# Seven products instead of eight for more weight pairs, with two of the four weight sums made by transfers in DRAM

## The chip, the cores and the metric

One core of a Trainium2 chip runs the whole program. The metric is the device time of one execution in microseconds (us). The engines: TensorE (PE, its weight loads listed as PEld), VectorE (DVE), ScalarE (ACT), GpSimd (POOL) and SyncE (SP), each with an instruction queue of its own that it works off in order. Here nearly all DMAs that load weights are issued by SP, the others by POOL.

## The reference

One layer of a decoder trunk on x of 256 tokens x 2048, all in float32:

```
h  = rmsnorm(x);  z = h @ w_in          # q, k, v, gates of both kinds of heads
A  = forgetting attention (8 heads);  M = mLSTM (4 heads)
x  = x + (sigmoid(g_a) * (A @ w_proj_a) + sigmoid(g_m) * (M @ w_proj_m)) @ w_out
h2 = rmsnorm(x);  u = causal_dwconv(h2 @ w_up)      # 2 x 5632 columns
x  = x + (silu(u_gate) * u_val) @ w_down            # 5632 -> 2048
```

## The kernel before, in words

*Precision.* Each float32 operand is split into a part `wh` that the matmul's input type holds and a rest `wl`. A product takes three matmuls: rest x wh, high x wh, high x wl (`prod`, L302). The splitting of the weights runs while the matmuls run: ACT copies a piece of up to 1024 columns into `wh` (L176), DVE subtracts to get `wl` (L177). Both have four buffers (L174, L175).

*Loading.* All weight matrices are one list of chunks [128, up to 2048], loaded by SP in that order into three buffers `raw` (`load_chunk`, L130). `subs_of` cuts each chunk into pieces; `split_sub(j)` (L140) makes piece j, `next_sub` (L184) hands it to the matmuls and splits one to three pieces ahead of them. The up product, the queries and the keys use chunks with two "whole" pieces.

*Pairs of seven products.* The products with the values (`w_v`, two blocks of 1024 columns), all gates (`w_g`, four blocks), the output weight (`w_out`, two) and the last product (`w_dn`, two blocks named y0 and y1) go by pairs of 128 contraction rows: 2 x 128 rows, 2 x 128 tokens and 2 x 512 columns make a 2 x 2 block product (`s_block`, L295). A pair of kind "p" does it with eight products of three matmuls, a pair of kind "S" with seven, by the Strassen-Winograd scheme: sums of the four weight blocks and sums of the four activation blocks come in, sums of the products come out. The pattern of a block is a string (L36 to L39): "pSpSpSpp" for eight pairs, "p" + "Sp" * 10 + "p" for the 22 pairs of the last product.

For an S pair the four weight sums are made on DVE from the loaded chunk: a wide one of 1024 columns (L161, both halves at once), then two of 512 (L168, L171). Its pieces are b (1024 columns), b21 (512), t13 and t24 (1024 each, out of the sums), and the matmuls take them in that order, 6, 3, 6 and 6 matmuls.

*Sums of the activations.* They are made once (`put_sums`, L226). For the values and gates they stay in SBUF (`sums`, L638, done during the key product); for the last product they are written to DRAM during the up product (L961) and come back in a ring of tiles `s_ops` for two pairs each (L971), on POOL's queue.

*Order.* The code's order is the order of each engine's queue except where the tool that builds the program finds an instruction ready earlier in its own estimate of the times, and queues it ahead. `tc.issue_after(x)` keeps what follows behind x on that engine's queue (used at L160 and L507).

*End of a block.* The seven products of all S pairs accumulate in PSUM over the block; after the last S pair DVE and ACT combine them two operations per piece (`late`, L308), then the block's four quarters are finished and stored (L999), from SP's queue.

Of the kernel before, what the change touches and what calls it, by code (L numbers as in the profile page):

```python
# [14 lines left out]
ALU = mybir.AluOpType  # L15
# [17 lines left out]

V_PAIRS = "pSpSpSpp"  # L36
G_PAIRS = "pSpSpSpp"
WO_PAIRS = "pSpSpSpp"
Y_PAIRS = "p" + "Sp" * 10 + "p"  # L39
N_S = Y_PAIRS.count("S")  # L40

# [22 lines left out]
def trunk(ctx: ExitStack, tc: tile.TileContext, a):  # L66
# [41 lines left out]
        add_chunk(a["w_mog0"][i], 2 * (MOG[0] + MOG[1]))  # L108
    add_b(a["w_mog1"], MOG[2])

    def add_pairs(ap, patterns):
        for i, kind in enumerate("".join(patterns)):
            pieces = ("b", "b21", "t13", "t24") if kind == "S" else ("whole", "whole")
            add_chunk(ap[i], 2048, pieces)

# [8 lines left out]
    subs_of[n + 1], subs_of[n + 2] = subs_of[n + 2], subs_of[n + 1]  # L124
    add_pairs(a["w_dn"], [Y_PAIRS] * 2)

    raws, subs, s_tiles, last_of = {}, {}, {"of": None}, {}
    n_chunk = len(chunks)

    def load_chunk(i, part=None):  # L130
# [6 lines left out]
        c = slice(0, n) if part is None else slice(part * n // 2, (part + 1) * n // 2)  # L137
        nc.sync.dma_start(raws[i][:, c], src[:, c])

    def split_sub(j):  # L140
        if j >= len(subs_of) or j in subs:
            return
        i, s, kind = subs_of[j]
        load_chunk(i)
        if j < KD:
            put(hT[j][:, 0, :], hT[j][:, 1, :], xT[j], cst[:, C_G1 + j : C_G1 + j + 1])
        n = 512 if kind == "b21" else chunks[i][1] // 2
        raw, sums = raws[i], s_tiles.get("sums")


        if kind == "whole":
            src = raw[:, s * n : (s + 1) * n]
        elif kind == "b":
            src = raw[:, 512:1536]
            if s_tiles["of"] != chunks[i][2]:
                s_tiles["of"] = chunks[i][2]
                s_tiles["sums"] = a8(f"sums{i}", [2048])
            sums = s_tiles["sums"]

            with tc.issue_after(last_of["wl"].ins):  # L160
                nc.vector.tensor_tensor(  # L161
                    sums[:, :1024].rearrange("p (i c) -> p i c", i=2),
                    raw[:, :512].unsqueeze(1).to_broadcast([P, 2, 512]),
                    src.rearrange("p (i c) -> p i c", i=2), ALU.subtract,
                )
        elif kind == "b21":
            src = raw[:, 1536:]
            nc.vector.tensor_tensor(sums[:, 1024:1536], raw[:, 1024:1536], sums[:, :512], ALU.subtract)  # L168
        elif kind == "t13":
            src = sums[:, :1024]  # L170
            nc.vector.tensor_tensor(sums[:, 1536:], raw[:, 1536:], sums[:, 1024:1536], ALU.subtract)  # L171
        else:
            src = sums[:, 1024:]
        wh = wpool.tile([P, 1024], F32R, tag="wh", bufs=4, name=f"wh{j}")  # L174
        wl = wpool.tile([P, 1024], F32R, tag="wl", bufs=4, name=f"wl{j}")  # L175
        nc.scalar.activation(wh[:, :n], src, AF.Copy)  # L176
        last_of["wl"] = nc.vector.tensor_tensor(  # L177
            wl[:, :n], src, wh[:, :n].bitcast(F32), ALU.subtract
        )
        subs[j] = (wh[:, :n], wl[:, :n])  # L180
# [45 lines left out]
    def put_sums(src, dst, keep):  # L226

        a11, a21, a12, a22 = (src[:, i * P : (i + 1) * P] for i in range(4))  # L230
        n = 4 if keep else 3
        sv = scratch("sv", [P, n * P])
        s2, s3, s4 = (sv[:, i * P : (i + 1) * P] for i in range(3))
        s1 = sv[:, 3 * P :] if keep else a21
        nc.vector.tensor_tensor(s3, a21, a11, ALU.subtract)
        nc.vector.tensor_tensor(s1, a21, a22, ALU.add)
        nc.vector.tensor_tensor(s2, s1, a11, ALU.subtract)
        nc.vector.tensor_tensor(s4, a12, s2, ALU.subtract)
        put(dst[0], dst[1], sv)

    def mm(out, lhsT, rhs, start, stop):
# [53 lines left out]
    def s_block(name, pairs, s_ops, pattern, pools, dst, add=True, per_piece=0):  # L295


        q = [[pools[0](f"{name}q{tok}{h}") for h in range(2)] for tok in range(2)]
        ps, late, left = {}, [], pattern.count("S")
        n_s = left  # L300

        def prod(out, x, w, c, first, last):  # L302
            wh, wl = w[0][:, c * 512 : (c + 1) * 512], w[1][:, c * 512 : (c + 1) * 512]
            mm(out, x[1], wh, first, False)
            mm(out, x[0], wh, False, False)
            mm(out, x[0], wl, False, last)

        def piece():  # L308
            w = next_sub(4)
            for _ in range(min(2, len(late))):  # L310
                late.pop(0)()
            run_tasks(per_piece)
            return w

        def tt(o, x, y):
            late.append(lambda: nc.vector.tensor_tensor(o, x, y, ALU.add))

        for m, kind in enumerate(pattern):
            def op(i, tok):
                t = slice(tok * P, (tok + 1) * P)  # L320
                return pairs[m][:, i, 0, t], pairs[m][:, i, 1, t]

            if kind == "p":
                last = m == len(pattern) - 1
                ws = [piece(), piece()] if last else []

                todo = (
                    [(i, tok, h) for h in range(2) for tok in range(2) for i in range(2)] if last
                    else [(i, tok, h) for i in range(2) for h in range(2) for tok in range(2)]
                )  # L330
                for i, tok, h in todo:
                    if i == len(ws):
                        ws.append(piece())
                    prod(q[tok][h], op(i, tok), ws[i], 1 - h, m == 0 and i == 0, last and i == 1)
                continue
            first, last = left == n_s, left == 1
            left -= 1
            s1, s2, s3, s4 = s_ops[m]
            w = piece()
            if first:  # L340
                ps = {i: pools[1](f"{name}p{i}") for i in (1, 5, 7, 6)}
            prod(ps[1], op(0, 0), w, 0, first, last)
            prod(q[0][1], s4, w, 1, False, False)
            prod(q[0][0], op(1, 0), piece(), 0, False, False)
            w = piece()
            prod(ps[5], s1, w, 0, first, last)
            prod(ps[7], s3, w, 1, first, last)
            w = piece()
            prod(ps[6], s2, w, 0, first, last)
            prod(q[1][0], op(1, 1), w, 1, False, False)  # L350
            if not last:
                continue
            c11, c12, c21, c22 = (dst(tok, h) for tok in range(2) for h in range(2))
            ps = {i: like(x, c11) for i, x in ps.items()}
            u2 = like(scratch("u2", [P, 512]), c11)
            if add:
                u3 = scratch("u3", [P, 512])
                late.append(lambda: nc.scalar.activation(u2, ps[1], AF.Copy))
                tt(c11, c11, ps[1])
                tt(u2, u2, ps[6])  # L360
                tt(u3, u2, ps[7])
                tt(u2, u2, ps[5])
                tt(c21, c21, u3)
                tt(u3, u3, ps[5])
                tt(c12, c12, u2)
                tt(c22, c22, u3)
            else:
                late.append(lambda: nc.scalar.activation(c11, ps[1], AF.Copy))
                tt(u2, c11, ps[6])
                tt(c21, u2, ps[7])  # L370
                tt(c12, u2, ps[5])
                tt(c22, c21, ps[5])
        for f in late:
            f()
        return q
# [36 lines left out]
    upper = const.tile([P, P], F32, name="upper")  # L412
    ones = const.tile([P, P], F32, name="ones")
    mhalf = const.tile([P, 8], F32, name="mhalf")
    mask_qk = const.tile([P, P], BF16, name="mask_qk")
    mask_st = const.tile([P, P], BF16, name="mask_st")

# [4 lines left out]

    def when_there(x):

        return nc.gpsimd.tensor_copy(mhalf[:, :1], x[:, :1].bitcast(F32))

    def make_constants():
        nc.gpsimd.memset(mhalf, -0.5)
# [190 lines left out]


    hN, hN_pairs = operand("hN")
    n_sums = [m for m, kind in enumerate(V_PAIRS) if kind == "S"]
    n_ops = {}

    def whole(pair):
# [319 lines left out]
    for j in range(NF):  # L945
# [9 lines left out]
        if j % 2 == 0:  # L955
            continue
        m = j // 2
        if Y_PAIRS[m] == "S":
            se = big.tile([P, 2, 3 * P], F32R, tag="mv", name=f"se{m}")
            put_sums(gv, (se[:, 0], se[:, 1]), False)  # L960
            nc.gpsimd.dma_start(  # L961
                s_dram[:, n_s * 6 * P : (n_s + 1) * 6 * P], se.rearrange("p l c -> p (l c)")
            )
            n_s += 1
        put_pair(g_pairs[m], gv)


    s_pos = [m for m, kind in enumerate(Y_PAIRS) if kind == "S"]
    ring = []

    def load_sums():  # L971
# [14 lines left out]
    for b in range(2):  # L986
# [7 lines left out]
        for h in range(2):  # L994
            for tok in range(2):
                v = dst(tok, h)
                nc.vector.tensor_tensor(v, v, q[tok][h], ALU.add)
                c = c0 + h * 512
                nc.sync.dma_start(a["out"][tok * P : (tok + 1) * P, c : c + 512], v)  # L999


def _blocks(w, n, kt=4):
# [74 lines left out]
```

## Time and profile before

| what | us |
|---|---|
| median of three runs (1371.94 to 1372.09) | 1372.03 |
| the profiled execution, its own time | 1372.16 |
| its span, first to last instruction | 1370.0 |
| PE busy | 1361.1 |
| DVE busy | 1122.7 |
| ACT busy | 784.3 |

The granted TensorE clock is 1.000 over the span. The span is what the trace shows, the time also holds what lies around it. A line of a group of instructions gives the busy time in total and the mean of one in ns, then the engine's idle time just before them and what ended it. Busy time of PE is a union over overlapping matmuls, so the mean of one is longer than the step from one to the next.

### The profile page before, as it was taken

The page shows a single profiled execution, that of the slowest core. Times are in us where ns is not written, and L with a number is a line of the kernel's source. Part 1 is how long each engine was busy: PE and PEld are TensorE (multiplying, and loading weights), DVE is VectorE, ACT ScalarE, POOL GpSimd, SP SyncE. Part 2 cuts the span into 40 slices and gives each one's busy share as a digit, 9 for nine tenths or more (in the row PEclk, how much of TensorE's full clock was granted, in tenths as well). Part 3 has the DMA queues.
Part 4 walks back from the last instruction along what each step waited for, and adds up shares of the span by engine and source line. Part 5 has one row for each costly group of instructions (what it writes and reads, how often), then busy time and mean ns, then how long its engine had stood idle before and what let it go on. Part 6 is the DMA issues. An engine that isn't in the chain of part 4 may idle for free.

```text
span 1370.0 us, 18477 instructions
## 1 busy us (share of the span) xinstructions
PE 1361.1 (99%) x6907; PEld 1155.8 (84%) x6907; DVE 1122.7 (82%) x1600; ACT 784.3 (57%) x1116; POOL 40.9 (3%) x73
## 2 busy tenths in 40 slices
PE   9999999999999999999999999999999999999998
PEld 8878888888888888888888888888888888888887
DVE  5678888678988777999888888888888789889887
ACT  6756655446565644656656555555655555555553
POOL 2101000000000000000000000000000000000000
PEclk9999999999999999999999999999999999999999
DMA  8644555345555556465555555555555566767753
GB/s 324 239 158 181 196 207 212 130 147 215 213 188 202 180 184 224 162 236 206 204 196 201 192 206 205 197 185 196 203 201 194 205 227 234 257 234 284 295 188 121
DMA packets 44073, 281.76 MB, mean 206 GB/s; under 512 B 5008, under 2 KB 5024, under 8 KB 13264
## 3 DMA queue, kind: packets, MB, share of 16 engines
q1 hardware_dynamic: 39168, 260.20, 52.9%
q0 software_dynamic: 4672, 20.38, 4.3%
q8 instruction: 54, 0.88, 0.2%
q14 instruction: 35, 0.29, 0.1%
q10 hardware_dynamic: 144, 0.02, 0.0%
HBM read 272.45 MB, written 8.13 MB: 205 GB/s over the span
## 4 chain that ended last, share of the span: by engine, by line
PE 97%; issue 1%; DMA 1%; POOL 1%; DVE 0%; ACT 0%; SPq 0%; DVEq 0%; ACTq 0%; POOLq 0%
PE up L242 36%; PE p L242 6%; PE y1q L242 6%; PE y0q L242 6%; PE fq L242 3%; PE fk L242 3%; PE wo0q L242 2%; PE g0q L242 2%; PE g3q L242 2%; PE g2q L242 2%; PE g1q L242 2%; PE mvq L242 2%; PE fvq L242 2%; PE wo1q L242 2%; PE y1p L242 2%; PE y0p L242 2%
## 5 line engine op out<-in xcount | busy, mean ns | idle before, releaser
L176 ACT ACTIVATE wh<-raw 128x1024 fp32r<-128x1024 f32 (+2 forms) x496 | 493.2, 1009 | 359.7 <-PE up L242 109.3
L177 DVE TENSOR_TENSOR wl<-raw,wh 128x1024 fp32r<-128x1024 f32 (+2 forms) x496 | 567.9, 1157 | 136.2 <-ACT wh L176 131.6
L242 PE MATMUL up<-h,wh 128*128 128x512 f32 x1408 | 442.6, 396 | 0.0
L242 PEld LDWEIGHTS up<-h,wl 128*128 128x128 f32 x1408 | 264.4, 188 | 62.4
L242 PE MATMUL up<-h,wl 128*128 128x256 f32 x1408 | 276.6, 278 | 0.0
L242 PEld LDWEIGHTS up<-h,wh 128*128 128x128 f32 x1408 | 214.6, 189 | 0.4 <-DVE h L211 0.2
L176 ACT ACTIVATE wh<-sums 128x1024 fp32r<-128x1024 f32 x88 | 93.7, 1065 | 148.2 <-PE y1q L242 35.8
L177 DVE TENSOR_TENSOR wl<-sums,wh 128x1024 fp32r<-128x1024 f32 x88 | 107.5, 1222 | 54.3 <-ACT wh L176 54.2
L933 DVE SCALAR_TENSOR_TENSOR t<-u,cst,t 128x256 f32<-128x256 f32 x176 | 84.8, 482 | 3.7 <-ACT t L931 0.7
L242 PE MATMUL p<-wh,am 128*128 128x512 f32 x256 | 81.1, 397 | 0.0
L242 PE MATMUL y0q<-wh,ghl 128*128 128x512 f32 x232 | 71.5, 389 | 0.0
L242 PE MATMUL y1q<-wh,ghl 128*128 128x512 f32 x232 | 71.5, 389 | 0.0
L242 PEld LDWEIGHTS p<-wh,am 128*128 128x128 f32 x256 | 47.3, 188 | 9.5
L161 DVE TENSOR_TENSOR sums<-raw 128x1024 f32<-128x1024 f32 x44 | 53.6, 1219 | 0.0
L931 ACT ACTIVATE t<-u,cst 128x256 f32<-128x256 f32 x88 | 52.2, 594 | 1.7 <-DVE u L928 1.7
L242 PEld LDWEIGHTS y1q<-wh,ghl 128*128 128x128 f32 x232 | 43.5, 188 | 9.0
L242 PEld LDWEIGHTS y0q<-wh,ghl 128*128 128x128 f32 x232 | 43.5, 188 | 9.0
L242 PE MATMUL p<-wl,am 128*128 128x512 f32 x128 | 50.0, 391 | 0.0
L242 PE MATMUL y0q<-wl,ghl 128*128 128x512 f32 x116 | 45.1, 389 | 0.0
L242 PE MATMUL y1q<-wl,ghl 128*128 128x512 f32 x116 | 45.1, 389 | 0.0
L242 PE MATMUL mog<-wh,hT 128*128 128x348 f32 (+1 forms) x192 | 41.1, 323 | 2.1 <-ACT wh L176 1.7
L242 PE MATMUL fq<-wh,hT 128*128 128x512 f32 x128 | 40.0, 394 | 0.0
(418 smaller groups left out, 2050.5 us busy)
## 6 DMA issues: line engine op xcount, KB each, us to landing
raw<-in_w_up SPq DMA_DIRECT2D x88, 1024.0 KB, 4.8
raw<-in_w_dn SPq DMA_DIRECT2D x44, 1024.0 KB, 4.9
raw<-in_w_g SPq DMA_DIRECT2D x32, 1024.0 KB, 4.8
raw<-in_w_fox SPq DMA_DIRECT2D x16, 1024.0 KB, 4.9
raw<-in_w_v SPq DMA_DIRECT2D x16, 1024.0 KB, 4.8
raw<-in_w_p SPq DMA_DIRECT2D x16, 1024.0 KB, 4.9
raw<-in_w_out SPq DMA_DIRECT2D x16, 1024.0 KB, 4.8
raw<-in_w_mqk SPq DMA_DIRECT2D x8, 1024.0 KB, 4.9
```

What stands on the lines that cost most here:

```text
L161: nc.vector.tensor_tensor(sums[:, :1024].rearrange("p (i c) -> p i c", i=2), raw[:, :512].unsqueeze(1).to_broadcast([P, 2, 512]), src.rear ...
L176: nc.scalar.activation(wh[:, :n], src, AF.Copy)
L177: last_of["wl"] = nc.vector.tensor_tensor(wl[:, :n], src, wh[:, :n].bitcast(F32), ALU.subtract)
L242: last_of["mm"] = nc.tensor.matmul(out, lhsT, rhs, start=start, stop=stop)
L931: nc.scalar.activation(t, u[:, 2:], AF.Identity, scale=w[2], bias=w[3])
L933: nc.vector.scalar_tensor_tensor(out=t, in0=u[:, i : i + S], scalar=w[i], in1=t, op0=ALU.mult, op1=ALU.add)
```

## The change

A third kind of pair, "H", has seven products like S, but two of its four weight sums are made in DRAM, by two transfers on POOL's queue: one writes a block of the weight twice into a new DRAM tile t of 1024 columns, the second adds two other blocks into it. An H pair is then two chunks for SP: 1536 columns of the weight and the 1024 of t. Its pieces: h (1024, the weight as it is), h21 (512), h13 (the first chunk of sums as loaded) and h24, for which DVE makes two sums of 512 columns. The matmuls take 6, 3, 6 and 6 of them as in S.

The patterns of values and gates become "pSHpSHpp" and that of the last product "pp" + "SHp" * 5 + "SpHpp"; the output weight keeps its own. To each H pair's two transfers `plan` gives a time: at the first piece of certain chunks of an earlier product (the values' during queries and keys, the gates' from the third chunk of the values on, in groups of two pairs and steps four chunks apart; the last product's during the up product, one pair at a time, steps three chunks apart). There ACT copies one column of `wh`, POOL copies that (`when_there`), and the transfers are queued behind it. Since a transfer can add but not subtract, the signs of the scheme are turned: weight sums by additions, activation sums and some of the final combinations by subtractions. And the stores of the last product's first half go out on POOL's queue.

```diff
-V_PAIRS = "pSpSpSpp"
-G_PAIRS = "pSpSpSpp"
+V_PAIRS = "pSHpSHpp"
+G_PAIRS = "pSHpSHpp"
-Y_PAIRS = "p" + "Sp" * 10 + "p"
+Y_PAIRS = "pp" + "SHp" * 5 + "SpHpp"
...
+            if kind == "H":
+                t = dram.tile([P, 1024], F32, name=f"t{len(h_sums)}")
+                h_sums.append((t, ap[i]))
+                add_chunk(ap[i][:, 512:], 1536, ("h", "h21"))
+                add_chunk(t, 1024, ("h13", "h24"))
+                continue
...
+    def plan(source, beside, apart, group):
+        c0 = next(i for i, c in enumerate(chunks) if c[2] == a[beside].tensor.name) + 2
+        mine = [i for i, (_, w) in enumerate(h_sums) if w.tensor.name == a[source].tensor.name]
+        for n, i in enumerate(mine):
+            for step in range(2):
+                c = c0 + apart * (2 * (n // group) + step)
+                j = next(j for j, x in enumerate(subs_of) if x[0] == c)
+                steps_at.setdefault(j, []).append((i, step))
+
+    plan("w_v", "w_fox", 4, 2)
+    plan("w_g", "w_v", 4, 2)
+    plan("w_dn", "w_up", 3, 1)
...
+    def begin_steps(j, x):
+        mark = marks[:, list(steps_at).index(j) :][:, :1]
+        nc.scalar.activation(mark, x[:, :1].bitcast(F32), AF.Copy)
+        with tc.issue_after(when_there(mark).ins):
+            for i, step in steps_at[j]:
+                t, w = h_sums[i]
+                if step:
+                    nc.gpsimd.dma_start(t, w[:, 512:1536], accum_op=ALU.add)
+                else:
+                    b12 = w[:, :512].unsqueeze(1).to_broadcast([P, 2, 512])
+                    nc.gpsimd.dma_start(t.rearrange("p (i c) -> p i c", i=2), b12)
...
-                    src.rearrange("p (i c) -> p i c", i=2), ALU.subtract,
+                    src.rearrange("p (i c) -> p i c", i=2), ALU.add,
                 )
+        elif kind in ("h", "h13"):
+            src = raw[:, :1024]
+        elif kind == "h21":
+            src = raw[:, 1024:1536]
+        elif kind == "h24":
+            b, src = raws[i - 1], sums[:, 1024:]
+            nc.vector.tensor_tensor(src[:, :512], b[:, 512:1024], raw[:, :512], ALU.add)
+            nc.vector.tensor_tensor(src[:, 512:], b[:, 1024:1536], src[:, :512], ALU.add)
...
         nc.scalar.activation(wh[:, :n], src, AF.Copy)
+        if j in steps_at:
+            begin_steps(j, wh)
...
-                nc.sync.dma_start(a["out"][tok * P : (tok + 1) * P, c : c + 512], v)
+                q_out = nc.gpsimd if b == 0 else nc.sync
+                q_out.dma_start(a["out"][tok * P : (tok + 1) * P, c : c + 512], v)
```

More of the change, by code (lines that the diff above doesn't have):

```diff
@@ L31 @@
 MOG = (348, 346, 346)
-V_PAIRS = "pSpSpSpp"
-G_PAIRS = "pSpSpSpp"
+V_PAIRS = "pSHpSHpp"
+G_PAIRS = "pSHpSHpp"
 WO_PAIRS = "pSpSpSpp"
-Y_PAIRS = "p" + "Sp" * 10 + "p"
-N_S = Y_PAIRS.count("S")
+Y_PAIRS = "pp" + "SHp" * 5 + "SpHpp"
+N_S = len(Y_PAIRS) - Y_PAIRS.count("p")
 PROJ = ("w_proj_a", "w_proj_m")
@@ L109, in trunk @@
     add_b(a["w_mog1"], MOG[2])
+    h_sums = []
     def add_pairs(ap, patterns):
         for i, kind in enumerate("".join(patterns)):
+            if kind == "H":
[4 more added lines that the diff above has]
+                continue
             pieces = ("b", "b21", "t13", "t24") if kind == "S" else ("whole", "whole")
@@ L125, in trunk @@
     add_pairs(a["w_dn"], [Y_PAIRS] * 2)
+    steps_at = {}
+    def plan(source, beside, apart, group):
[9 more added lines that the diff above has]
+    plan("w_dn", "w_up", 3, 1)
+    marks = const.tile([P, len(steps_at)], F32, name="marks")
+    def begin_steps(j, x):
[9 more added lines that the diff above has]
+                    nc.gpsimd.dma_start(t.rearrange("p (i c) -> p i c", i=2), b12)
     raws, subs, s_tiles, last_of = {}, {}, {"of": None}, {}
@@ L138, in load_chunk, with source_of @@
         nc.sync.dma_start(raws[i][:, c], src[:, c])
+    def source_of(i):
+        return chunks[i][2]
     def split_sub(j):
@@ L146, in split_sub @@
             put(hT[j][:, 0, :], hT[j][:, 1, :], xT[j], cst[:, C_G1 + j : C_G1 + j + 1])
-        n = 512 if kind == "b21" else chunks[i][1] // 2
+        n = {"whole": chunks[i][1] // 2, "b21": 512, "h21": 512}.get(kind, 1024)
+        if kind in ("b", "h") and s_tiles["of"] != source_of(i):
+            s_tiles["of"] = source_of(i)
+            s_tiles["sums"] = a8(f"sums{i}", [2048])
         raw, sums = raws[i], s_tiles.get("sums")
@@ L154, in split_sub @@
             src = raw[:, 512:1536]
[L155 to L158, printed above, removed]
             with tc.issue_after(last_of["wl"].ins):
@@ L163, in split_sub @@
                     raw[:, :512].unsqueeze(1).to_broadcast([P, 2, 512]),
-                    src.rearrange("p (i c) -> p i c", i=2), ALU.subtract,
+                    src.rearrange("p (i c) -> p i c", i=2), ALU.add,
                 )
+        elif kind in ("h", "h13"):
[6 more added lines that the diff above has]
+            nc.vector.tensor_tensor(src[:, 512:], b[:, 1024:1536], src[:, :512], ALU.add)
         elif kind == "b21":
             src = raw[:, 1536:]
-            nc.vector.tensor_tensor(sums[:, 1024:1536], raw[:, 1024:1536], sums[:, :512], ALU.subtract)
+            nc.vector.tensor_tensor(sums[:, 1024:1536], raw[:, 1024:1536], sums[:, :512], ALU.add)
         elif kind == "t13":
             src = sums[:, :1024]
-            nc.vector.tensor_tensor(sums[:, 1536:], raw[:, 1536:], sums[:, 1024:1536], ALU.subtract)
+            nc.vector.tensor_tensor(sums[:, 1536:], raw[:, 1536:], sums[:, 1024:1536], ALU.add)
         else:
@@ L234, in put_sums @@
         s1 = sv[:, 3 * P :] if keep else a21
-        nc.vector.tensor_tensor(s3, a21, a11, ALU.subtract)
-        nc.vector.tensor_tensor(s1, a21, a22, ALU.add)
+        nc.vector.tensor_tensor(s3, a11, a21, ALU.subtract)
+        nc.vector.tensor_tensor(s1, a21, a22, ALU.subtract)
         nc.vector.tensor_tensor(s2, s1, a11, ALU.subtract)
-        nc.vector.tensor_tensor(s4, a12, s2, ALU.subtract)
+        nc.vector.tensor_tensor(s4, a12, s2, ALU.add)
         put(dst[0], dst[1], sv)
@@ L298, in s_block @@
         q = [[pools[0](f"{name}q{tok}{h}") for h in range(2)] for tok in range(2)]
-        ps, late, left = {}, [], pattern.count("S")
+        ps, late, left = {}, [], len(pattern) - pattern.count("p")
         n_s = left
@@ L313, in piece, with tt @@
             return w
-        def tt(o, x, y):
-            late.append(lambda: nc.vector.tensor_tensor(o, x, y, ALU.add))
+        def tt(o, x, y, op=ALU.add):
+            late.append(lambda: nc.vector.tensor_tensor(o, x, y, op))
         for m, kind in enumerate(pattern):
@@ L361, in s_block @@
                 tt(u3, u2, ps[7])
-                tt(u2, u2, ps[5])
+                tt(u2, ps[5], u2, ALU.subtract)
                 tt(c21, c21, u3)
-                tt(u3, u3, ps[5])
+                tt(u3, ps[5], u3, ALU.subtract)
                 tt(c12, c12, u2)
@@ L370, in s_block @@
                 tt(c21, u2, ps[7])
-                tt(c12, u2, ps[5])
-                tt(c22, c21, ps[5])
+                tt(c12, ps[5], u2, ALU.subtract)
+                tt(c22, ps[5], c21, ALU.subtract)
         for f in late:
@@ L414, in trunk @@
     mhalf = const.tile([P, 8], F32, name="mhalf")
+    seen = const.tile([P, 1], F32, name="seen")
     mask_qk = const.tile([P, P], BF16, name="mask_qk")
@@ L423, in when_there @@
     def when_there(x):
-        return nc.gpsimd.tensor_copy(mhalf[:, :1], x[:, :1].bitcast(F32))
+        return nc.gpsimd.tensor_copy(seen, x[:, :1].bitcast(F32))
     def make_constants():
@@ L621, in trunk @@
     hN, hN_pairs = operand("hN")
-    n_sums = [m for m, kind in enumerate(V_PAIRS) if kind == "S"]
+    n_sums = [m for m, kind in enumerate(V_PAIRS) if kind != "p"]
     n_ops = {}
@@ L957, in trunk @@
         m = j // 2
-        if Y_PAIRS[m] == "S":
+        if Y_PAIRS[m] != "p":
             se = big.tile([P, 2, 3 * P], F32R, tag="mv", name=f"se{m}")
@@ L965, in trunk @@
         put_pair(g_pairs[m], gv)
-    s_pos = [m for m, kind in enumerate(Y_PAIRS) if kind == "S"]
+    s_pos = [m for m, kind in enumerate(Y_PAIRS) if kind != "p"]
     ring = []
```

## The prediction

> **What bounds the kernel now.** I read the page first (engines, chain), then the busy times by stage, the chain in order of time inside a pair product, the groups by form, short timelines of PE, ACT and DVE, and last the DMAs. From the page:
>
> ```profile
> span 1370.0 us, 18477 instructions
> ...
> PE 1361.1 (99%) x6907; PEld 1155.8 (84%) x6907; DVE 1122.7 (82%) x1600; ACT 784.3 (57%) x1116; POOL 40.9 (3%) x73
> ...
> PE 97%; issue 1%; DMA 1%; POOL 1%; DVE 0%; ACT 0%; SPq 0%; DVEq 0%; ACTq 0%; POOLq 0%
> ```
>
> PE is never idle for long and the chain that ends last is 97% PE. So a matmul taken away shortens the span, as long as no other engine, buffer or queue turns late. What is near to late shows by stage (columns: PE, PEld, DVE, ACT, POOL busy, clock, DMA share, GB/s):
>
> ```profile
> 102.70:148.30 45.60, 45.60 (x210) 37.54 (x209) 39.29 (x63) 26.78 (x55) 4.03 (x4) 1.00 0.53 195
> 148.30:231.30 83.00, 83.00 (x367) 68.71 (x367) 70.66 (x81) 46.42 (x60) 2.01 (x2) 1.00 0.57 205
> 293.50:459.00 165.50, 165.50 (x733) 137.06 (x732) 140.82 (x153) 96.30 (x107) 0.00 (x0) 1.00 0.56 201
> 648.00:1140.00 492.00, 491.99 (x2825) 429.17 (x2824) 405.60 (x655) 291.98 (x440) 8.58 (x14) 1.00 0.56 201
> 1140.00:1254.00 114.00, 114.00 (x504) 94.40 (x503) 101.66 (x112) 64.51 (x70) 3.17 (x6) 1.00 0.71 253
> ```
>
> The rows are: keys; values; gates; up product; first half of the last product. In every one PE is busy from end to end, with DVE second at 82 to 89%. One period of the last product (a seven-product pair, then a whole pair) in the chain:
>
> ```profile
> 1179.86 6.12 PE y0q L242 x27
> 1186.66 1.36 PE y0q L242 x6
> 1188.02 2.04 PE y0p L242 x9
> 1190.06 6.12 PE y0q L242 x27
> ```
>
> The period is 1190.06 - 1179.86 = 10.20 us. It holds 27 + 6 + 9 matmuls and three more in the 0.68 us between the first two rows, 45 in all (24 for p, 21 for S): 0.2267 us a matmul, with no gap.
>
> **The change part by part.**
>
> *Matmuls.* Per column block, values and gates go from three to four pairs of seven products, the last product from ten to twelve: 2 x 1 + 4 x 1 + 2 x 2 = 10 pairs more, one product of three matmuls less in each: 30 matmuls. The groups:
>
> ```profile
> L177 DVE TENSOR_TENSOR wl<-raw,wh 128x1024 fp32r<-128x1024 f32 x428 | 517.0, 1222 | 129.2 <-ACT wh L176 124.9
> L176 ACT ACTIVATE wh<-raw 128x1024 fp32r<-128x1024 f32 x428 | 447.2, 1061 | 341.8 <-PE up L242 108.1 <-issue 79.4 <-PE p L242 34.3
> L242 PE MATMUL y0q<-wh,ghl 128*128 128x512 f32 x232 | 71.5, 389 | 0.0
> L161 DVE TENSOR_TENSOR sums<-raw 128x1024 f32<-128x1024 f32 x44 | 53.6, 1219 | 0.0
> L168 DVE TENSOR_TENSOR sums<-raw,sums 128x512 f32<-128x512 f32 x44 | 30.1, 684 | 0.0
> L171 DVE TENSOR_TENSOR sums<-raw,sums 128x512 f32<-128x512 f32 x44 | 30.1, 684 | 0.0
> L208 DVE TENSOR_TENSOR se<-sv,se 128x384 fp32r<-128x384 f32 x10 | 5.5, 550 | 0.0
> L235 DVE TENSOR_TENSOR sv<-gv 128x128 f32<-128x128 f32 x13 | 3.8, 290 | 0.4
> ```
>
> The mean of one matmul, 389 ns, overlaps its neighbours; 30 x 0.389 = 11.7 us would be wrong. By the step it is 30 x 0.2267 = **-6.8 us**, all on the path. The Trainium skill, "TensorE: Matmul & The Clock Gate" (Back-to-back issue gap), gives a lower sustained spacing, about 131 ns for 512 columns in a stream of weight loads and matmuls; by that the 30 would be an estimated 3.9 us. The trace of these same matmuls differs, at 227 ns, and decides.
>
> *DVE work per pair.* Timelines of PE, ACT and DVE in the last product:
>
> ```profile
> 1183.10 0.62 PE L242 MATMUL y0q<-wh,ghl 128*128 128x512 f32 x2
> 1183.12 1.07 ACT L176 ACTIVATE wh<-sums 128x1024 fp32r<-128x1024 f32 x1 [2.13 <-PE y0q L242]
> 1185.82 0.62 PE L242 MATMUL y0p<-wh,ghl 128*128 128x512 f32 x2
> 1185.84 1.06 ACT L176 ACTIVATE wh<-sums 128x1024 fp32r<-128x1024 f32 x1 [1.65 <-PE y0q L242]
> 1186.94 1.23 DVE L177 TENSOR_TENSOR wl<-sums,wh 128x1024 fp32r<-128x1024 f32 x1 [1.27 <-ACT wh L176]
> 1191.71 1.22 DVE L177 TENSOR_TENSOR wl<-raw,wh 128x1024 fp32r<-128x1024 f32 x1
> 1192.85 0.69 DVE L168 TENSOR_TENSOR sums<-raw,sums 128x512 f32<-128x512 f32 x1
> 1193.45 0.68 DVE L177 TENSOR_TENSOR wl<-raw,wh 128x512 fp32r<-128x512 f32 x1
> ```
>
> Back to back, DVE takes 1.14 us for 1024 columns and 0.60 for 512. S: one wide and two narrow sums, three wide wl and a narrow one, 4 x 1.14 + 3 x 0.60 = 6.4 us. H has no wide sum: 5.2 us. p: 2.3 us. S H p is 13.9 us of DVE against 66 x 0.2267 = 14.96 us of PE, 93%, where S p is 8.7 of 10.20, 85%. On average DVE keeps up; what it has to spare shrinks.
>
> *The wait in H.* The same rows give the rhythm: four wh buffers, so a wh starts when PE begins the piece three before it (1185.84 after 1185.82; 1183.12 after 1183.10), and its wl 1.10 us after that. Take an H behind an S, zero at H's first matmul, DVE in the order of the code. S's t24 begins 6 matmuls earlier, at -1.36; wh of h13 at -1.34, its wl at -0.24, leaving DVE free at 0.90; the two new sums end at 1.50 + 0.69 = 2.19; wh of h24 at 2.2, its wl from 3.3 to 4.53. PE wants it at the third matmul of h24, 17 matmuls in, at 3.85. That is 0.68 us late. Behind a p, the piece three before h13 begins 12 matmuls before H, everything is 1.36 earlier, and nothing waits. There are 2 x 2 + 4 x 2 + 2 x 5 = 22 pairs H behind S, so the bound is 22 x 0.68 = +15.0 us. Put both sums ahead of wl of h13, into the time in which DVE waits: by the same steps wl of h21 leaves DVE at -0.54, wl of h13 runs 0.66 to 1.88 (wanted at 2.49), wl of h24 ends at 3.1: no wait, bound 0. One sum ahead: 0.38 late. Which it is, no row of before shows. The nearest are these, from the start of the values:
>
> ```profile
> 145.11 1.22 DVE L161 TENSOR_TENSOR sums<-raw 128x1024 f32<-128x1024 f32 x1
> 146.36 0.69 DVE L168 TENSOR_TENSOR sums<-raw,sums 128x512 f32<-128x512 f32 x1
> 146.97 1.22 DVE L177 TENSOR_TENSOR wl<-raw,wh 128x1024 fp32r<-128x1024 f32 x1
> ```
>
> The code has L177 between L161 and L168; the program built from it has the sum L168 ahead. So instructions that are ready are queued past ones that wait, and the next pair's matmuls could be queued past a late third one too. I take the near end, 0.05 a pair: **+1.1 us**, with 0 and 15.0 kept.
>
> *Sums in DRAM.* 24 H pairs, two POOL transfers each: the first writes 512 KB from 256, the second adds 512 KB into it. 36 small ACT and POOL copies time them. POOL is busy 40.9 us of the span, ACT 57%; these hide, and POOL's other work (gate norms, s_ops loads) stands behind a mark that is already past in program order. What does not hide is the traffic:
>
> ```profile
> raw<-in_w_v SPq DMA_DIRECT2D x12, 1024.0 KB, 4.8
> raw<-in_w_dn SPq DMA_DIRECT2D x18, 1024.0 KB, 6.4
> s_ops<-s_dram POOLq DMA_DIRECT2D x5, 768.0 KB, 6.8
> xs<-x POOLq DMA_DIRECT2D x4, 512.0 KB, 4.1
> xr<-xs POOLq DMA_DIRECT2D x2, 1024.0 KB, 7.8
> SPq L138 <- DVE wl L177: 57.9, 11, 6.1
> ```
>
> Beside 768 KB from POOL a weight load lands in 6.4 us, alone in 4.8: 1.6 us more. No row moves DRAM to DRAM or adds: I bound one transfer by 4.1 and 7.8 us, and what a step (two transfers) does to a load by 1.6 and, for a megabyte read twice, 1.6 x 2048/768 = 4.3 us. Beside keys, queries and the up product it costs nothing: SP itself waits for buffers (last row), loads are asked for two chunks ahead, 492 us / 88 = 5.6 us each. In an S H p run the next S is asked for when H's second sum ends, 2.2, lands at 7.0, its wl is done 2.4 later at 9.4 and wanted at 45 + 2 matmuls, 10.65: 1.3 us to spare. 1.6 then costs 0.3, 4.3 costs 3.0. Of the steps for the gates three fall on an H (chunks 2 and 6 of the values, 2 of the gates), the rest on p pairs or the mqk product. Bounds 0 and 9.0; I take three times 0.3: **+0.9 us**. The ring of last-product operands is loaded once per S H p, 15 us, instead of 20.4, up to half a pair before it is wanted: 0, at most 0.3 x 10 = 3.0.
>
> *Nothing:* the fourth operand sum of the values (about 4 x 0.29 + 3 x 0.68 = 3.2 us of DVE) hides in the keys' 45.60 - 39.29 = 6.3 us of idle DVE; two more of the last product's (4 x 0.29 + 0.55 each) in the up product's 86 us. Signs cost nothing. Results of the first half leave from POOL: SP's loads no longer stand behind four of them, but PE had no gap there; behind them on POOL stand the second half's xr, which reuses their buffer anyhow, and a ring load that is wanted a whole S H p later.
>
> Sum: -6.8 + 1.1 + 0.9 = -4.8 us. The profiled execution is 1372.16 us (span 1370.0 and 2.16 around it), 0.13 over the median of the runs, 1372.03. 1372.16 - 4.8 = **1367.4 us**.
>
> **The rivals.**
> *The late sum (slower).* The order of the code holds and each H behind S waits 0.68 us: 1372.16 - 6.8 + 15.0 = 1380.4 us. It decides from 6.8 / 22 = 0.31 us a pair. For it: the worked chain, and in 1191.71 to 1193.45 DVE runs in code order. Against: the rows at 145 to 147.
> *The traffic.* The three steps beside an H cost some 2 us each, between 0.3 and 3.0: 1372.16 - 6.8 + 6.0 = 1371.4 us, no change. For it: 6.4 against 4.8. Against: 1.3 us to spare, and DMA shares of 0.57 and 0.56 there.
> *The sums come too late.* Should a transfer in DRAM take more than the three chunks between steps (16.8 us), H's load waits and PE with it; twelve H pairs late by 1 us or more give 1377 or worse. The bound of 7.8 speaks against it.
>
> **How the numbers follow.** About 0.2% (2.7 us) is what a measurement here tells from no change. Forecast 0.55 (1365.4 with no wait to 1369.4), traffic 0.20, late sum 0.20, sums too late 0.05. That gives faster 0.55, same 0.20, slower 0.25. The range starts at 1365.0, a little under the full 6.8, and runs to 1379.0, where a late sum with some pairs spared still lies. The forecast's own range is 1365.0 to 1369.4.
>
> **What would show it.** PE should have 30 matmuls less, the period S H p 14.96 us in the chain. DVE in H: two 512 sums; ahead of wl of h13 if I am right. If the late sum holds, "wl" of the fourth piece of H ends PE's idle time, 0.7 us at a time. If the traffic: raw loads of w_v over 7 us, and PE idle behind wh. Wrong altogether if PE's share falls under 98% in the up product.

## The result, and the profile after

The changed kernel takes 1389.8 us (median, 1387.6 to 1390.3; the kernel before on the same chip 1372.04): ratio 1.0126, 95% interval 1.0109 to 1.0144. It is 17.8 us slower, where 1367.4 was forecast; the time lies outside the range. The profiled execution took 1389.4 us. From its page: the span, the engines, and the engines' shares of the chain that ends last.

```profile
span 1387.6 us, 18727 instructions
...
PE 1368.3 (99%) x6877; PEld 1147.4 (83%) x6877; DVE 1141.2 (82%) x1642; ACT 799.6 (58%) x1175; POOL 102.6 (7%) x165
...
PE 88%; DVE 4%; DMA 4%; ACT 2%; issue 1%; SPq 0%; ACTq 0%; DVEq 0%
```

The matmuls are 30 fewer (6877 after 6907), as intended. But the chain was 97% PE and is 88% PE: DVE, DMA and ACT hold 10% of it. Stage by stage (values; mqk product; gates; first half of the last product; columns as before):

```profile
148.30:241.30 93.00, 86.92 (x360) 66.97 (x359) 74.49 (x87) 47.81 (x66) 11.88 (x17) 0.98 0.75 239
241.30:302.80 61.50, 61.50 (x383) 53.83 (x382) 41.95 (x98) 29.27 (x67) 4.77 (x6) 1.00 0.59 187
302.80:474.40 171.60, 167.86 (x726) 134.56 (x725) 149.16 (x170) 101.57 (x118) 2.73 (x3) 1.00 0.61 217
1155.00:1268.00 113.00, 112.45 (x491) 91.14 (x490) 101.61 (x115) 65.56 (x73) 4.25 (x8) 1.00 0.75 271
```

PE was busy for all of the values' 83.0 us; now it is idle for 6 of 93. The stage has grown by more than these 6 us: up to 0.16 us of each wait counts as busy (a matmul is shown 0.39 us long where the step to the next is 0.23), and one stretch ran at half clock (last section). The mqk product between values and gates is as full as it was. The length of each stage, from its first matmul to the next stage's first, in us (fvq and mvq are the two halves of the values; "ahead" and "moved" are the runs sums_ahead and gates_sums_moved below):

| stage | before | after | ahead | moved |
|---|---|---|---|---|
| queries, keys | 47.73, 45.58 | 47.70, 45.49 | 47.71, 45.49 | 47.71, 45.49 |
| fvq | 41.48 | 50.83 | 49.52 | 41.34 |
| mvq | 41.48 | 42.61 | 41.77 | 40.80 |
| mqk product | 61.07 | 61.31 | 61.39 | 61.04 |
| first gate block | 42.28 | 46.78 | 45.63 | 41.60 |
| each later gate block | 41.48 | 41.59 | 40.80 | 40.80 |
| up product | 491.61 | 491.58 | 491.61 | 491.58 |
| last product, halves | 112.89, 112.65 | 113.69, 114.39 | 111.55, 112.49 | 111.55, 112.24 |

Three matmuls fewer in each added pair of seven products (one such pair more a block, two in each half of the last product) make 40.80 of 41.48 and 111.53 of 112.89. Against these lengths the changed kernel loses two things of different shape: a little in every block with H pairs (0.79 in each gate block, 2.16 in the first half of the last product), and much in two places, 9 to 10 us in fvq and about 5 in the first gate block (mvq loses 1.8).

*The little one.* The chain in the last product, one S H p:

```profile
1188.83 1.24 DVE wl L232
...
1190.61 5.96 PE y0q L297 x26
...
1202.01 1.15 PE y0q L297 x5
1203.16 1.07 ACT wh L229
...
1204.26 1.24 DVE wl L232
```

Once in each period the chain leaves PE for wh and wl of the fourth piece of H, and the period is 1204.26 - 1188.83 = 15.43 us for 66 matmuls of 0.2267, 14.96. DVE at that place:

```profile
1200.63 0.68 DVE L217 TENSOR_TENSOR sums<-raw,raw 128x512 f32<-128x512 f32 x1
1201.23 1.22 DVE L232 TENSOR_TENSOR wl<-raw,wh 128x1024 fp32r<-128x1024 f32 x1
1202.37 0.68 DVE L218 TENSOR_TENSOR sums<-raw,sums 128x512 f32<-128x512 f32 x1
1204.26 1.23 DVE L232 TENSOR_TENSOR wl<-sums,wh 128x1024 fp32r<-128x1024 f32 x1 [1.21 <-ACT wh L229]
```

L217 and L218 are the two sums of H. One stands ahead of the third wl, the other behind it: neither the code's order nor the one that the forecast took.

*The large one.* The chain in fvq, and DVE and PE where it returns to them:

```profile
160.15 8.80 DMA raw<-in_w_v
...
169.06 1.07 ACT wh L229
```

```profile
160.05 0.68 DVE L218 TENSOR_TENSOR sums<-raw,sums 128x512 f32<-128x512 f32 x1
161.91 1.22 DVE L232 TENSOR_TENSOR wl<-sums,wh 128x1024 fp32r<-128x1024 f32 x1 [1.19 <-ACT wh L229]
163.06 2.35 DVE L232 TENSOR_TENSOR wl<-raw,wh 128x1024 fp32r<-128x1024 f32 x2
168.98 1.23 DVE L205 TENSOR_TENSOR sums<-raw 128x1024 f32<-128x1024 f32 x1 [3.57 <-DMA raw<-in_w_v]
```

```profile
169.25 0.39 PE L297 MATMUL fvq<-wl,hN 128*128 128x512 f32 x1
170.18 0.73 PE L297 MATMUL fvp<-wh,hN 128*128 128x512 f32 x2 [0.54 <-ACT wh L229]
171.44 0.50 PE L297 MATMUL fvp<-wl,hN 128*128 128x512 f32 x1 [0.53 <-DVE wl L232]
```

The load of the next S is asked for at 160.15, when the second sum of H is being made and H's first chunk gives up its buffer. PE wants it behind its matmul of 169.25, some 9.3 us later. Two transfers for the gates had begun at 156.8 and 157.5; the load took 8.80 us instead of 4.8. The answer on DMAs for the two value blocks (kind, count, size, median us to landing):

```profile
t<-in_w_g POOLq DMA_DIRECT2D x10, 512.0 KB, 9.2
raw<-in_w_mqk SPq DMA_DIRECT2D x4, 1024.0 KB, 9.8
raw<-in_w_v SPq DMA_DIRECT2D x3, 768.0 KB, 6.0
raw<-t SPq DMA_DIRECT2D x3, 512.0 KB, 8.8
```

### The profile page after: what moved, and what is told of

Read it like the earlier page. It is cut to its first block, busy times and chain, and to the rows that moved or that the text cites. A ratio compares the mean times of both kernels' runs of the same rounds, so it can differ in the third digit from the quotient of the medians.

```text
span 1387.6 us, 18727 instructions
## 1 busy us (share of the span) xinstructions
PE 1368.3 (99%) x6877; PEld 1147.4 (83%) x6877; DVE 1141.2 (82%) x1642; ACT 799.6 (58%) x1175; POOL 102.6 (7%) x165
## 4 chain that ended last, share of the span: by engine, by line
PE 88%; DVE 4%; DMA 4%; ACT 2%; issue 1%; SPq 0%; ACTq 0%; DVEq 0%
PE up L297 35%; PE p L297 6%; PE y0q L297 6%; PE y1q L297 5%; PE fq L297 3%; PE fk L297 3%; DVE wl L232 3%; PE mog L297 3%; PE wo0q L297 2%; PE g2q L297 2%; PE g1q L297 2%; PE g3q L297 2%; PE y0p L297 2%; PE y1p L297 2%; ACT wh L229 2%; PE mq L297 2%
## 5 line engine op out<-in xcount | busy, mean ns | idle before, releaser
L229 ACT ACTIVATE wh<-raw 128x1024 fp32r<-128x1024 f32 (+3 forms) x520 | 510.5, 1000 | 406.7 <-PE up L297 130.1
L232 DVE TENSOR_TENSOR wl<-raw,wh 128x1024 fp32r<-128x1024 f32 (+3 forms) x520 | 590.0, 1149 | 137.0 <-ACT wh L229 134.6
L229 ACT ACTIVATE wh<-sums 128x1024 fp32r<-128x1024 f32 x84 | 89.1, 1060 | 108.6 <-DVE sums L218 27.6
L232 DVE TENSOR_TENSOR wl<-sums,wh 128x1024 fp32r<-128x1024 f32 x84 | 102.6, 1222 | 47.3 <-ACT wh L229 46.2
L297 PE MATMUL y0q<-wh,ghl 128*128 128x512 f32 x208 | 65.0, 390 | 0.0
L297 PE MATMUL y1q<-wh,ghl 128*128 128x512 f32 x208 | 65.0, 390 | 0.0
L483 POOL COPY seen<-marks 128x1 f32<-128x1 f32 x36 | 20.5, 570 | 430.6 <-ACT marks L158 430.6
L205 DVE TENSOR_TENSOR sums<-raw 128x1024 f32<-128x1024 f32 x30 | 36.5, 1217 | 8.9 <-DMA raw<-in_w_g 4.4
L297 PE MATMUL y1q<-wl,ghl 128*128 128x512 f32 x104 | 40.5, 390 | 0.0
L297 PE MATMUL y0q<-wl,ghl 128*128 128x512 f32 x104 | 40.5, 389 | 0.0
```

The costliest lines, as they stand in the source:

```text
L205: nc.vector.tensor_tensor(sums[:, :1024].rearrange("p (i c) -> p i c", i=2), raw[:, :512].unsqueeze(1).to_broadcast([P, 2, 512]), src.rear ...
L232: last_of["wl"] = nc.vector.tensor_tensor(wl[:, :n], src, wh[:, :n].bitcast(F32), ALU.subtract)
L297: last_of["mm"] = nc.tensor.matmul(out, lhsT, rhs, start=start, stop=stop)
L483: return nc.gpsimd.tensor_copy(seen, x[:, :1].bitcast(F32))
```

## The experiments

Two theories stood to be told apart for each loss. For the small one: the late second sum, or a DVE that is too full. For the large one: transfers in DRAM that stretch the loads beside them, or the H pairs by themselves.

**Both sums ahead (sums_ahead).** The sums move to the third piece and are held ahead of its wl:

```
        elif kind == "h13":
            b, src, late = raws[i - 1], raw[:, :1024], sums[:, 1024:]
            with tc.issue_after(last_of["wl"].ins):
                nc.vector.tensor_tensor(late[:, :512], b[:, 512:1024], raw[:, :512], ALU.add)
                after = nc.vector.tensor_tensor(late[:, 512:], b[:, 1024:1536], late[:, :512], ALU.add)
...
        with tc.issue_after(after.ins) if kind == "h13" else nullcontext():
            last_of["wl"] = nc.vector.tensor_tensor(wl[:, :n], src, wh[:, :n].bitcast(F32), ALU.subtract)
```

> Both sums of H's fourth piece are made ahead of wl of h13, and kept there. Theory (second sum queued behind wl of h13, 0.4 us at each of the 22 H behind an S, the other loss being the transfers for the gates): the period S H p in the last product goes from 15.40 to 14.96 us, the time falls by about 8.8 us, from 1389.8 to some 1381; a little more if the raw buffers that come free earlier help the loads. Rival (VectorE has no time left in S H p, wherever the sums stand): the period stays near 15.4 and the time within 1 us of 1389.8.

Measured: 1380.25 us, 9.55 less than the changed kernel (ratio to before 1.0066, 1.0049 to 1.0082). The chain in its last product:

```profile
1183.96 6.12 PE y0q L302 x27
...
1195.52 1.36 PE y0q L302 x6
1196.88 2.04 PE y0p L302 x9
1198.92 6.12 PE y0q L302 x27
```

The chain stays on PE from one period to the next, 1198.92 - 1183.96 = 14.96 us, with the same DVE work. So it was the order and not DVE's load. DVE in that H:

```profile
1194.14 0.69 DVE L217 TENSOR_TENSOR sums<-raw,raw 128x512 f32<-128x512 f32 x1
1194.86 0.69 DVE L218 TENSOR_TENSOR sums<-raw,sums 128x512 f32<-128x512 f32 x1
1195.47 1.22 DVE L237 TENSOR_TENSOR wl<-raw,wh 128x1024 fp32r<-128x1024 f32 x1
1196.77 1.23 DVE L237 TENSOR_TENSOR wl<-sums,wh 128x1024 fp32r<-128x1024 f32 x1
```

The fourth wl now stands right behind the third; the 1.21 us in which DVE waited for wh are gone.

**Both sums behind (sums_behind).** The two additions held behind the third wl, the order of the code:

```
+            with tc.issue_after(last_of["wl"].ins):
                 nc.vector.tensor_tensor(src[:, :512], b[:, 512:1024], raw[:, :512], ALU.add)
```

> Both sums are kept behind wl of h13, the order in which the code has them. Theory: each H behind an S waits 0.68 us instead of 0.4, so the period in the last product is 15.64 us and the time grows by some 22 x 0.25 = 5.5 us, to about 1395. Rival (VectorE's total work is what counts): no change, 1389.8.

Measured: 1391.33 us (ratio 1.0138, 1.0123 to 1.0154): 1.5 over the changed kernel, not 5.5, and the runs of the two overlap (1389.29 to 1392.19 here). The later gate blocks are 41.62 long, 0.41 lost per H and not 0.68. PE in a gate block, at the fourth piece of H, shows why:

```profile
362.88 0.73 PE L298 MATMUL g1p<-wh,ns 128*128 128x512 f32 x2
363.45 0.88 PE L298 MATMUL g1q<-wh,hN 128*128 128x512 f32 x3
364.17 0.47 PE L298 MATMUL g1p<-wl,ns 128*128 128x512 f32 x1
```

H's first matmul was at 359.39; its 18th was due at 359.39 + 17 x 0.2267 = 363.24 and ran at 364.17, 0.93 late. But three matmuls of the next pair stand ahead of it in PE's queue, where the program that was built had put them, and use 0.68 of that time. What is left, 0.25, and matmuls that follow each other more slowly around it make the 0.41.

**No H in the gates (gates_no_h).** The gates take "pSppSppp" (two S a block instead of four of eight by seven products), and the values' H pairs stay; with them go all transfers beside the values.

> The gates' blocks go back to two S pairs and six whole pairs each, without H pairs and without their transfers; values and last product as in the change. Theory (the gates' transfers beside the values delay the weight loads): the product with the values, 93.4 us in the change, falls to 82.96 - 1.36 + 4 x 0.4 = 83.2 us; the first gates block has no gap. The gates themselves lose 8 pairs of seven products, 8 x 0.68 = 5.4 us, and their waits; the whole lands near 1380. Rival (two chunks per H pair on three raw buffers are too few without any transfers): the values' product stays above 90 us.

Measured: 1378.11 us (ratio 1.0043, 1.0027 to 1.0059). The values take 42.60 + 41.74 = 84.3 us instead of 93.4, with their four H pairs unchanged. The whole is 1.9 us under the 1380 that was expected. The last product keeps its losses (113.64, 114.91).

**Transfers alone (transfers_only).** The patterns of before; all 48 transfers are issued at their times, and nothing reads the results.

> The patterns of the kernel before, with no H pair at all, but the 48 transfers in DRAM are issued at the planned chunks; nothing reads their result. Theory that the transfers alone cost: the values' product grows by some 5 us or more over its 82.96, the last product stays, the time is 1377 or more. Theory that they cost only together with H's short reserve of loaded chunks: the values' product stays within 1 us and the time within 1.5 us of 1372.0.

Measured: 1371.15 us (ratio 0.9994, 0.9984 to 1.0003), every stage as before. The transfers cost nothing beside S and p pairs. A stretch of 93 us from the start of the values in this run (some 10 us of it already the mqk product) and in sums_ahead, one row of each:

```profile
148.10:241.10 93.00, 93.00 (x434) 77.55 (x433) 79.16 (x97) 51.68 (x75) 15.45 (x17) 1.00 0.78 248
```

```profile
148.30:241.30 93.00, 87.38 (x372) 69.31 (x371) 76.83 (x90) 49.82 (x68) 12.47 (x17) 0.98 0.78 247
```

The DMA engines are as busy (0.78) and move as much (248 and 247 GB/s) in both. PE is idle for nothing in the first and for 5.6 us in the second, so the traffic alone isn't the cause. And the load beside the first step of transfers, asked for at 158.67 in transfers_only, is slower than that of the changed kernel:

```profile
raw<-in_w_v SPq DMA_DIRECT2D x1, 1024.0 KB, 10.1
```

PE wants it here at 173.42, 14.8 us after it was asked for. In the changed kernel 9.3 us were not enough for 8.80.

**The last product only (last_product_only).** Sums ahead, values and gates as before ("pSpSpSpp", no sums in DRAM).

> Values and gates as in the kernel before (three of eight, no sums in DRAM for them); only the last product has twelve of 22 pairs by seven products, with both sums of H ahead of the third wl, and its 24 transfers beside the up product. Theory (transfers in DRAM cost only where they run beside H pairs, and the up product has cover): every stage up to the up product as before, fvq 41.5; first half of the last product 111.55, second half 112.5 as in the run with both sums ahead; 1372.04 - 1.35 - 0.15 = 1370.5 us. Rival (the transfers for the last product, twelve pairs in 491 us, cost something after all once H is used): up product over 491.6 and 1372 or more.

Measured: 1369.45 us (ratio 0.9982, 0.9974 to 0.9991), up product 491.59, halves 111.55 and 112.57. The 24 transfers beside the up product cost nothing.

**The gates' sums elsewhere (gates_sums_moved).** From sums_ahead, one line; every H pair and every transfer is kept:

```
-    plan("w_g", "w_v", 4, 2)
+    plan("w_g", "w_mqk", 1, 2)
```

> As the run with both sums ahead, but the gates' sums are made beside the mqk product and the first chunks of the gates instead of beside the values; all H pairs are kept. Theory (the 8.7 us over in the values are raw loads stretched by transfers that run at the same time): fvq near 41.5, mvq 40.8, about 1380.25 - 9 = 1371 us, unless the mqk product (61.4 us) or the first gate block takes part of it back. Rival (H pairs by themselves run the values short of loaded chunks): fvq stays near 49.5 and the time near 1380.

Measured: 1365.79 us (1365.63 to 1365.95), ratio 0.9954 (0.994 to 0.9968): 14.46 us less than sums_ahead, 24.0 less than the changed kernel, and faster than the kernel before by 6.3 us. The values, the mqk product (which now has the transfers beside it), the gates and the first half of the last product:

```profile
148.30:230.40 82.10, 81.90 (x362) 67.49 (x361) 74.99 (x88) 48.63 (x63) 2.04 (x2) 1.00 0.62 224
230.40:291.40 61.00, 61.00 (x381) 53.61 (x380) 42.07 (x99) 29.03 (x72) 16.96 (x23) 1.00 0.90 249
291.40:456.00 164.60, 164.60 (x729) 136.32 (x728) 150.82 (x170) 102.42 (x118) 0.83 (x1) 1.00 0.64 228
1136.00:1248.00 112.00, 112.00 (x495) 92.73 (x495) 103.90 (x115) 66.52 (x74) 5.17 (x10) 1.00 0.75 277
```

In the mqk product the DMA share is 0.90, the highest of all these rows, and PE is busy for the whole 61.00 us. The time is 5 us better than expected, since mvq (41.77 to 40.80) and the first gate block (45.63 to 41.60) came back too.

The loads of the mqk product are stretched as well. The last of them, asked for at 255.16, and PE's first matmul on it:

```profile
raw<-in_w_mqk SPq DMA_DIRECT2D x1, 1024.0 KB, 9.2
```

```profile
284.22 0.71 PE L302 MATMUL mk<-hN,wh 128*128 128x512 f32 x2
```

It took 9.2 us, longer than the load of 160.15 in the changed kernel, but PE wanted it 29 us after it was asked for, and no wait follows.

**One sum at a time (gates_sums_single).** From sums_ahead, beside the values again, `plan("w_g", "w_v", 2, 1)`: half the burst, twice as often.

> As the run with both sums ahead, but each step beside the values makes one sum instead of two, every second chunk instead of every fourth: the same bytes in the same stage, in half the burst. If what counts is how long one burst holds up a load behind it (two transfers: loads of 8.8 to 11.7 us; one: about 6.5 to 7), fvq falls to 43 to 45 and the time to about 1375. If what counts is the bytes moved in the stage, fvq stays near 49.5 and the time near 1380.

Measured: 1375.53 us (1373.36 to 1378.18; ratio 1.0027, 1.0018 to 1.0036). fvq 44.77, mvq 43.67, first gate block 43.79: of the 14.5 us, 4.7 are gone, as was expected of the smaller burst. mvq is 1.9 us longer than in sums_ahead, so a part of the loss only moved. The transfers also begin at other chunks now, and this run can't tell the size of a burst from its place.

**One H a block (one_h_a_block).** "pSpSpSHp" for values and gates, sums ahead, the six sums made beside queries and keys: all thirty matmuls saved with half the sums there.

> All thirty matmuls saved with half the sums in DRAM: each block of values and gates has three S and one H (p S p S p S H p), the last product as in the run with both sums ahead; the six sums of values and gates are all made beside queries and keys, none beside the values or gates. Theory (late sums and transfers beside H were the whole loss): fvq, mvq and the four gates near 40.8 each (first gate 41.6), last product 111.55 and 112.5, 1372.04 - 6.8 + 1.0 = 1366.2 us. Rival (an H also delays the S that is loaded behind it, without any transfer beside it): 0.5 to 1 us more in each of six blocks, 1369 to 1372.

Measured: 1366.83 us (ratio 0.9963, 0.9951 to 0.9976); fvq 41.19, the other blocks 40.94 to 40.95. The later blocks are 0.14 longer than with "pSHpSHpp", fvq 0.15 shorter. The 0.5 to 1 us a block of the rival are not there.

**The order kept, the sums elsewhere (sum_order_kept).** The changed kernel with only the `plan` line of gates_sums_moved.

> The changed kernel with its own order of DVE (one sum of H ahead of the third wl, one behind), and with the gates' sums made beside the mqk product instead of beside the values. If the two losses add (late sums 9.55 us, stretched loads 14.5 us): values and gate blocks at 41.6, last product 113.7 and about 114.4, 1389.8 - 14.5 = 1375.3 us. If the late sum only shows because loads are late as well, the blocks fall to 40.8 without any change of the order and the time to about 1366.

Measured: 1376.67 us (ratio 1.0038, 1.0023 to 1.0053). The two losses add, nearly: the later gate blocks stay at 41.59, and fvq falls to 42.61, 1.0 more than expected. With the transfers moved first and the sums put ahead second, the steps bring 13.1 and 10.9 us; the other way round the sums bring 9.55 and the transfers 14.46. The profiled execution, 1379.27 us, is the slowest of four (the others 1376.60 to 1376.68): its last product takes 114.71 and 117.07, more than the 113.7 and 114.4 that were expected, and that is not explained.

**H set apart from the next S (h_set_apart).** From sums_ahead, "pSHppSHp" for values and gates.

> As the run with both sums ahead, with the gates' transfers beside the values as they were, but the pairs of values and gates in the order p S H p p S H p: two whole pairs (10.9 us of PE) between an H and the next S instead of one (5.4 us). Matmuls, bytes and transfers are the same. Theory (what is lost is an S asked for only when the H before it gives up its buffer, 9.3 us before PE wants it, where 14.8 us were enough): at least half of the 14.5 us goes, fvq 45 or less, 1372 us or less. Rival (too many bytes at once for the DMA engines in this stage): fvq near 49.5, time near 1380.

Measured: 1385.46 us (ratio 1.0096, 1.0079 to 1.0113), fvq 49.57: the expectation failed. It was wrong about which load is late. The DMA answer for the load asked for at 159.42, when H gives up its buffer, and ACT behind it:

```profile
raw<-in_w_v SPq DMA_DIRECT2D x1, 1024.0 KB, 10.7
```

```profile
170.18 2.01 ACT L233 ACTIVATE wh<-raw 128x1024 fp32r<-128x1024 f32 x2 [7.77 <-DMA raw<-in_w_v]
```

This load now belongs to the second p behind H. PE was through with the first at 168.7, again 9.3 us after the request. With three buffers it is always the third chunk after H's first that is asked for there; a different pair on that place changes nothing. The last H of the values now lies nearer to the end, and a load for the mqk product that took 11.97 us stands behind most of the 5.1 us that are added there (66.47 after 61.39); a stretch at half clock is in them too (last section).

## Why the prediction was wrong

*Matmuls: right.* 30 fewer at 0.2267 us. Where nothing else is late, the blocks lost 0.68 (41.48 to 40.80) and 1.34 us (112.89 to 111.55) as worked out.

*The wait in H: this step failed, by the value that was chosen.* It took 0.05 us a pair, since a sum stood ahead of its place in the program of before. The program built from the change moved only one of the two sums ahead. For that case the prediction had 0.38; between the changed kernel and sums_ahead the stages differ by 0.38 to 0.43 a pair (0.79 / 2, 2.14 / 5, 1.90 / 5), and 9.55 us over 22 pairs, 0.43 each, come back when both sums are held ahead. That is more than the 0.31 a pair from which the late-sum rival was to decide, though at less than its 0.68. The 0.68 itself was too much even in the code's order (0.41, sums_behind), because the order of PE's queue shifts too.

*Sums in DRAM: this step failed by its size, beyond its bound.* The count was right: three steps beside an H were named, two in fvq and one in the first gates, and there most of the loss is: in sums_ahead (49.52 - 40.80) / 2 = 4.4 us each and 45.63 - 41.60 = 4.0, where 0.3 was taken and 3.0 was the end. Another 1.0 us is lost in mvq, where nothing was forecast. The working of the reserve held (from 2.2 to 10.65, 8.45 us from request to use in the forecast; 9.3 measured). The price of a step did not: 1.6 us more for a load came from one 768 KB load beside it. A step is two transfers of 512 KB that read and write DRAM, and a megabyte beside them took 8.8 to 11.7 us in the changed kernel's fvq, 4.0 to 6.9 more than 4.8 where the bound was 4.3; one transfer took up to 12.6 us where the bound was 7.8. The loads behind are late as well, and up to 1.7 us of fvq's loss is a stretch of 3.41 us at half clock behind the waits (last section). The Trainium skill, "DMA: Bandwidth & Descriptors" (Issuing engines are not separate DMA queues), says that DMAs started by different engines run on the same 16 DMA engines and interleave. The trace agrees: transfers from POOL's queue stretched loads from SP's queue to 8.8 us and over.

*What was to cost nothing: right.* Keys, queries, up product and ACT and POOL copies cost nothing (transfers_only; stages in the table). The POOL ring and the stores were not tried by themselves; the second half of the last product stays 0.7 us over the first even in the best run (112.24 against 111.55), where the kernel before has 0.24 under. The trace of that run has it in one place: DVE waits 1.73 us for a weight load that lands at 1284.79 and then works without a gap, and PE waits 0.62 us for a wl, until 1295.71. That the one causes the other is not shown.

*The rivals.* Both the late sum (smaller than its price) and the traffic (larger) happened, and together: 1372.0 - 6.8 + 9.55 + 14.46 = 1389.2 of 1389.8 us. What this sum tests is that with both undone the kernel is within 0.6 us of 1372.04 - 6.8 = 1365.2. The third rival, sums that come too late, did not happen: no transfer in DRAM of the changed kernel took more than 12.6 us, under the 16.8 of three chunks. The prediction gave each a time as if only one could hold; a range that reached to both would have had to end near 1372.16 - 6.8 + 15.0 + 9.0 = 1389.4.

*Left open.* That the short time from request to use is what makes a stretched load cost something rests on the pair transfers_only and sums_ahead, on three traces with 9.3 or 14.8 us there, and on the stretched loads of the mqk product with 29 us. No run lengthens that time and leaves all else as it is, as a fourth buffer for raw would. Nor was the adding transfer priced apart from the plain one.

## What to carry over

A transfer "hidden" beside other work is paid where a load has little time between its request and its use: work out that time for every load from when its buffer comes free, and put extra traffic beside the stage where it is long, here the mqk product (the loads that the transfers stretched most were asked for 29 us ahead), even though the DMA engines are busiest there (0.90). Where a step's cost depends on the order in which an engine's queue was built, fix the order in the code instead of guessing it. When two rivals are independent of each other, the range must hold their sum.

## What was not expected of the hardware

Transfers within DRAM of 512 KB, issued in twos, landed after 6.3 to 9.4 us (the first) and 9.0 to 12.6 (the second) beside the values of the changed kernel; one at a time, in gates_sums_single, after 6.3 to 9.4. A 1 MB load beside them took 8.8 to 11.7 us in fvq, 1.8 to 2.4 times the 4.8 alone.

The clock of 0.98 in the values of the changed kernel, of sums_ahead and of h_set_apart is a mean. One stretch of 3.41 us ran at half clock, here in the changed kernel with the stretch of the same length before it (columns as before):

```profile
189.33:192.74 3.41, 1.91 (x6) 1.00 (x7) 2.62 (x3) 2.94 (x4) 0.00 (x0) 1.00 0.80 339
192.74:196.15 3.41, 3.41 (x9) 2.63 (x9) 3.41 (x5) 0.86 (x2) 1.94 (x3) 0.50 0.74 251
```

At 0.50 the matmuls follow each other in 0.43 us instead of 0.23, which makes some 1.6 us. PE's longest idle time before it was 1.6 us; in the 3.41 us ahead PE was busy for 1.91. Sums_ahead has such a stretch from 189.77, sums_behind from 172.68, h_set_apart from 190.79 and from 245.40. The best run, gates_sums_single and transfers_only have none in these stages. So a wait for a load can cost more than the idle time that the trace shows.
